# A decoder step on one core: the prompt's attention in units of two or four blocks of queries instead of single blocks

## The chip, the cores and the metric

The kernel is one program on one core of a Trainium2 chip. What counts is the time of the program on the device in microseconds (us), as the median of repeated runs. The engines are named as in the profile: PE is TensorE (matrix products and transposes; PEld is its loading of the stationary operand), DVE is VectorE, ACT is ScalarE, POOL is GpSimd, SP is SyncE (it issues the transfers).

## The reference

One layer of a decoder, for a prompt of 1024 tokens and 8 single sample tokens that share the weights, D_MODEL = 1024. The part that the change touches is the prompt's attention: 3 groups of 4 heads of 64 features, each with its own window and dilation.

```python
h = rms_norm(x, norm_mix_pre)
q, k, v, u, gates = jnp.split(h @ w_in, IN_SPLITS, axis=-1)
o, kv_bufs = attn_fn(q, k, v)
a = o.reshape(B, T, ATTN_OUT_W).astype(x.dtype) @ w_attn_out
c, conv_tail = conformer_conv(u, conv_hist, conv_w, conv_b, conv_ln_g, conv_ln_b, w_conv_out)
g = jax.nn.sigmoid(gates).reshape(B, T, 2, D_MODEL)
mix = (g[:, :, 0] * a + g[:, :, 1] * c) @ w_out
x = x + rms_norm(mix, norm_mix_post)
...
# band_dilated_attention, for each group (window, dilation): blocks of 128 queries,
# keys of the block itself and of the block before
s = jnp.einsum('bnqrhd,bnkrhd->bnrhqk', qb, kw) * SCALE + bias
s = jnp.where(valid[None, :, None, None], s, NEG)
lse = jax.nn.logsumexp(s, axis=-1)
pr = jnp.exp(s - lse[..., None])
o = jnp.einsum('bnrhqk,bnkrhd->bnqrhd', pr, vw)
```

After the mixing come a SwiGLU feed forward and an embedding gate; they take the second half of the time and are not touched.

## The kernel before

All big products keep f32 accuracy by splitting both operands into a high and a low part; `mm3` (lines 255 to 258) issues three products for each piece of 128 input features: L256 (high by high), L257 (low activations by high weights), L258 (high by low). `gemm_bank` fills one PSUM bank, 128 output features by one chunk of tokens, with 8 x 3 = 24 of these. The tokens come in three chunks `CH` of 384, 384 and 264 columns. So a "bank" below is 24 products of 384 or of 264 columns, and PE's work is a chain of banks.

Phase 1 (the first 500 us or so) makes the convolution's input (`u_pair`: 6 banks) and q, k, v for two heads at a time (`triple`: 9 banks; six triples, two for each of the three groups) in turns. A triple's attention runs beside the banks of the next steps. Its 8 blocks of 128 queries are each three steps (`attn_steps`):

- `qk`: the scores S of two heads, each into its own PSUM bank `S0`, `S1` (L592; the two heads lie on 64 partitions each), then on DVE bias and maximum (tile E from S) and on ACT the exponential (E from E),
- `pt`: the transposes of the probabilities, 128x128 each, into PSUM bank `PT` (L615), and ACT's copy to `PTs`,
- `pv`: the products with v into PSUM bank `O` (L630; each head uses 64 columns of the array), and ACT's copy to `oT`.

A block of group 0 or 1 that has a block before it has 256 keys (four transposes), the others 128 keys (two). The profile counts each f32 product of S and of O as two instructions, a transpose as one.

`attn_slot` is called after a bank, and on PE it puts three things next to each other: `pv` of the block two calls ago, `qk` of the new block, `pt` of the block one call ago. Such a stay of attention work between two products of a bank is called a visit below. There are 12 calls from one triple to the next; a triple needs 10. The last triple has only three banks left in `u_pair(7)`, so a loop after phase 1 issues the rest of its calls at once.

After phase 1 come 48 banks of the branch gates. Beside them, in a queue `bg` of generators that `pump` advances by a budget per bank, run the sample's attention, the rest of the convolution, `combine` (the three groups' results are read back from DRAM and weighted) and the convolution's layer norm. `misc()` hands out small PSUM banks from `mtags`, `bank()` the big ones from `gtags`.

PSUM has eight banks: three `g`, and `m`, `S0`, `S1`, `PT`, `O` with one buffer each. Scores, probabilities and small rows share a pool `sc` of four SBUF buffers. A scheduler places the instructions on each engine; the listings of order below show what it made.

Of the kernel before, what the change touches and what calls it, by code (L numbers as in the profile page):

```python
# [16 lines left out]
P = 128  # L17
# [9 lines left out]
# token chunks; the last holds 256 prompt tokens and the 8 sample tokens  # L27
# [9 lines left out]
# token chunks of the parts after the mix  # L37
# [17 lines left out]
def decoder_step(ctx: ExitStack, tc: tile.TileContext, ins, outs):  # L55
# [50 lines left out]
    class Engine:  # L106
        """An engine; its instructions stay in the order of emission while pinned[0] holds."""
# [59 lines left out]
    wq = []          # weight requests in the order of use: (dram view [128, n, 128], n)  # L167
# [75 lines left out]
    def finish(key):  # L243
        """The chains up to the one named."""
# [6 lines left out]
    def rng(c):  # L251
        """The token range of a chunk: its number among CH, or the range itself."""
# [7 lines left out]
    def gemm_bank(wi, xs, c, nk=KT, mid=None):  # L260
        """One bank: 128 output features by the tokens of chunk c."""
# [3 lines left out]
        for k in range(nk):  # L265
            if k == MID and mid is not None:
                mid()
# [7 lines left out]
    def gemm_bank_rows(wis, f, xs, c):  # L275
        """One bank, the weights held by rows: wis[k] has all output features of k."""
# [19 lines left out]
    def token_rstd(acc, c):  # L296
        """acc: SBUF [128, chunk] -> rstd columns of the tokens from the sums over the partitions."""
# [22 lines left out]
    class SumSq:  # L320
        """Sum of squares over feature tiles."""
# [25 lines left out]
    def split_scaled(src, g, hi, lo, c):  # L347
        """src * g per feature -> hi and lo."""
# [5 lines left out]
    def chunk_slots(name):  # L354
        """Four slots that hold a chunk of eight feature tiles, and the tiles' views."""
# [31 lines left out]
    # feed forward: the first tiles as they are, then pairs of gate and up  # L387
# [13 lines left out]
    # =====================================================================  # L401
    # start: loads, transposes, first norm, pp = p @ w_ple_proj
    # =====================================================================
# [44 lines left out]
    def setup():  # L448
# [25 lines left out]
        # relative position biases: table values by distance, as rows for skewed reads and as columns  # L474
# [41 lines left out]
        # biases of the sample's slots: the first 13 by distance, the tokens' own in every 16th row  # L516
# [55 lines left out]
    def o_view(o, g, blk):  # L572
        if g == 0:
            return o[:, blk * P:(blk + 1) * P]
        if g == 1:
            r, half = blk // 2, blk % 2
            return o[:, :S].rearrange("p (l r) -> p r l", r=4)[:, r, half * P:(half + 1) * P]
        j, r = blk // 4, blk % 4
        return o[:, :S].rearrange("p (l j i r) -> p j r i l", j=2, i=2, r=4)[:, j, r]

    def attn_steps(g, hp, qT, kT, vtok, oT, release):
        for blk in range(8):
            prev = (blk > 0) if g == 0 else (blk % 2 == 1) if g == 1 else False
            ko = 0 if prev else 128
            st = {}

            def qk(blk=blk, prev=prev, ko=ko, st=st):
                k0 = (blk - 1) * P if prev else blk * P
                nk = 256 - ko
                sp = [psa.tile([P, 512], F32, tag=f"S{h}", name=nm("S")) for h in range(2)]  # L590
                for h in range(2):
                    TE.matmul(sp[h][:, ko:256], qT[h * 64:(h + 1) * 64, blk * P:(blk + 1) * P],  # L592
                              kT[h * 64:(h + 1) * 64, k0:k0 + nk], start=True, stop=True)
                e = sc("E")
                for h in range(2):
                    head = hp * 2 + h
                    col = stat_col(g, blk, head)
                    if g < 2:
                        bv = biases[g][:, head * 256 + ko:(head + 1) * 256]
                    else:  # L600
                        bv = biases[g][:, head * P:(head + 1) * P]
                    ev = e[:, h * 256 + ko:(h + 1) * 256]
                    V.tensor_tensor_reduce(ev, sp[h][:, ko:256], bv, op0=ALU.add, op1=ALU.min,
                                           scale=-1.0, scalar=3e38, accum_out=NMs[g][:, col:col + 1])
                    A.activation(ev, ev, AF.Exp, scale=-1.0, bias=NMs[g][:, col:col + 1],
                                 accum_out=Ls[g][:, col:col + 1])
                st["e"] = e

            def pt(prev=prev, st=st):
                ps = psa.tile([P, 512], F32, tag="PT", name=nm("PT"))  # L610
                e = st["e"]
                for h in range(2):
                    for kb in range(0 if prev else 1, 2):
                        o = (h * 2 + kb) * P
                        TE.transpose(ps[:, o:o + P], e[:, o:o + P], ident)  # L615
                p = sc("PTs")
                if prev:
                    A.activation(p, ps, AF.Copy)
                else:
                    A.activation(p.rearrange("p (h b q) -> p h b q", h=2, b=2)[:, :, 1],  # L620
                                 ps.rearrange("p (h b q) -> p h b q", h=2, b=2)[:, :, 1], AF.Copy)
                st["p"] = p

            def pv(blk=blk, prev=prev, st=st):
                ps = psa.tile([P, 512], F32, tag="O", name=nm("O"))
                p = st["p"]
                kbs = range(0 if prev else 1, 2)
                for kb in kbs:
                    for h in range(2):
                        TE.matmul(ps[h * 64:(h + 1) * 64, :P], vtok[:, (blk - 1 + kb) * P + h * 64:(blk - 1 + kb) * P + (h + 1) * 64],  # L630
                                  p[:, (h * 2 + kb) * P:(h * 2 + kb + 1) * P],
                                  start=kb == kbs[0], stop=kb == kbs[-1])
                dst = o_view(oT, g, blk)
                src = ps[:, :P] if g < 2 else ps[:, :P].rearrange("p (i l) -> p i l", i=2)
                A.activation(dst, src, AF.Copy)
                if blk == 7:
                    SY.dma_start(d_o[g, hp], oT[:, :S])

            steps.append((qk, pt, pv))

    steps = deque()
    flight = deque()

    def attn_slot():
        new = steps.popleft() if steps else None
        if len(flight) > 1 and flight[1] is not None:
            flight[1][2]()
        if len(flight) > 1:
            flight.pop()
        if new is not None:  # L650
            new[0]()
        if flight and flight[0] is not None:
            flight[0][1]()
        flight.appendleft(new)

    def attn_busy():
        return bool(steps) or any(f is not None for f in flight)

# [1 line left out]
    def qkv_out(i):  # L660
        """The rows of the sample's tokens."""
# [12 lines left out]
    def kv_prompt_out(g, hp, dst, srcT):  # L674
        """The prompt's last rows, features by positions in the group's order."""
# [34 lines left out]
    def triple_done(i):  # L710
# [7 lines left out]
        attn_steps(g, hp, qT, kT, vtok, oT, None)  # L718
# [872 lines left out]
```

## Time and profile before

| | |
|---|---|
| time, median of 3 runs | 1733.48 us (1732.3 to 1733.5) |
| profiled execution, first to last instruction (span) | 1731.0 us |
| PE busy | 1712.0 us (99%) |
| DVE busy | 1220.9 us (71%) |
| ACT busy | 620.9 us (36%) |
| share of the chain that ended last | PE 96%, DVE 2%, issue 1% |

The profiled execution has no time of its own beside its span; the median of the timed runs lies 2.5 us above the span, which is what lies around the first and the last instruction. The chain that ended last is followed back from the end: 96% of it are PE's instructions, so time that PE gets free, or loses, is the kernel's time. A product's duration in the profile reaches from its start to its end in the pipeline, and neighbours overlap; what a product costs PE is the step from its start to the next start.

### The profile page before, as it was taken

What the parts mean: (1) busy time and instruction counts of PE and PEld (TensorE: products, weight loads), DVE (VectorE), ACT (ScalarE), POOL (GpSimd) and SP (SyncE); (2) the same over time, 40 slices, a digit from 0 to 9 for tenths busy, and PEclk for the clock granted to TensorE, in tenths of its full rate; (3) what the DMA queues carried; (4) which work ended last, traced back from release to release, by engine and by line L of the source; (5) the groups of instructions that cost most, each with busy time, mean ns of one, the idle gap of its engine ahead of it and who ended that gap; (6) DMA issues with size and microseconds to landing.
All of it is one profiled execution on the core that took longest, in us unless ns stands there. A gap on an engine that the chain in (4) does not pass through costs nothing.

```text
span 1731.0 us, 29699 instructions
## 1 busy us (share of the span) xinstructions
PE 1712.0 (99%) x12086; PEld 1661.9 (96%) x12086; DVE 1220.9 (71%) x2188; ACT 620.9 (36%) x1303; POOL 21.5 (1%) x29
## 2 busy tenths in 40 slices
PE   7999999999999999999999999999999999999999
PEld 7999998999989999999999999999999999999998
DVE  7899779858969696744577866666666545637863
ACT  6434434444352254323354432233332311213530
POOL 0000000000000000000000000000000000000000
PEclk9999999999999999999999999999999999999999
DMA  5231121121343322622252232233333532520411
GB/s 188 65 121 65 43 66 44 60 75 41 112 156 103 123 95 96 203 80 85 80 163 70 74 98 94 86 98 98 110 98 116 188 138 90 181 94 13 148 58 45
DMA packets 82254, 171.47 MB, mean 99 GB/s; under 512 B 11026, under 2 KB 52034, under 8 KB 81734
## 3 DMA queue, kind: packets, MB, share of 16 engines
q1 hardware_dynamic: 82118, 169.58, 29.8%
q8 instruction: 94, 1.54, 0.4%
q14 instruction: 42, 0.34, 0.1%
HBM read 133.04 MB, written 50.01 MB: 106 GB/s over the span
## 4 chain that ended last, share of the span: by engine, by line
PE 96%; DVE 2%; issue 1%; POOL 0%; DMA 0%; ACT 0%; POOLq 0%; SPq 0%; DVEq 0%
PE g L256 30%; PE g L258 30%; PE g L257 30%; PE S L592 1%; PE O L630 1%; PE PT L615 1%; DVE ogl L116 1%; PE m L317 0%; PE m L300 0%; PE m L690 0%; POOL r L116 0%; DVE acc L116 0%; DMA raw<-in_w_in_dram 0%; PE m L876 0%; DVE cs L116 0%
## 5 line engine op out<-in xcount | busy, mean ns | idle before, releaser
L256 PE MATMUL g<-hh,wh 128*128 128x384 f32 (+1 forms) x1200 | 393.3, 328 | 7.0 <-ACT wh L116 7.0
L257 PE MATMUL g<-hl,wh 128*128 128x384 f32 (+1 forms) x1200 | 386.6, 322 | 0.0
L258 PE MATMUL g<-hh,wl 128*128 128x384 f32 (+1 forms) x1200 | 386.3, 322 | 0.3 <-DVE wl L116 0.3
L116 DVE SCALAR_TENSOR_TENSOR y<-z,taps,y 128x1023 f32<-128x1023 f32 (+14 forms) x240 | 304.2, 1267 | 31.7 <-ACT y L116 26.1
L256 PEld LDWEIGHTS g<-hh,wh 128*128 128x128 f32 x1200 | 227.2, 189 | 10.7 <-ACT wh L116 7.0
L258 PEld LDWEIGHTS g<-hh,wl 128*128 128x128 f32 x1200 | 226.8, 189 | 1.5 <-DVE wl L116 0.8
L257 PEld LDWEIGHTS g<-hl,wh 128*128 128x128 f32 x1200 | 227.3, 189 | 0.9
L257 PE MATMUL g<-ul,wh 128*128 128x344 f32 x528 | 168.9, 320 | 0.0
L258 PE MATMUL g<-uh,wl 128*128 128x344 f32 x528 | 168.7, 320 | 0.0
L256 PE MATMUL g<-uh,wh 128*128 128x344 f32 x528 | 162.8, 320 | 0.6 <-DVE fa L116 0.6
L116 DVE TENSOR_TENSOR wl<-raw,wh 128x1024 fp32r<-128x1024 f32 x106 | 128.9, 1220 | 22.9 <-ACT wh L116 19.9
L116 DVE TENSOR_TENSOR pk<-pk,g 128x258 f32<-128x258 f32 x266 | 105.3, 420 | 52.4 <-PE g L258 36.9
L256 PE MATMUL g<-mh,wh 128*128 128x258 f32 x448 | 127.2, 285 | 0.0
L258 PE MATMUL g<-mh,wl 128*128 128x258 f32 x448 | 126.6, 283 | 0.0
L257 PE MATMUL g<-ml,wh 128*128 128x258 f32 x448 | 126.5, 283 | 0.0
L116 ACT ACTIVATE wh<-raw 128x1024 fp32r<-128x1024 f32 x106 | 110.7, 1052 | 6.5 <-DMA raw<-in_w_in_dram 4.2
L116 DVE TENSOR_TENSOR fa<-fa,g 128x344 f32<-128x344 f32 x96 | 47.1, 511 | 76.9 <-PE g L258 76.5
L258 PEld LDWEIGHTS g<-uh,wl 128*128 128x128 f32 x528 | 99.2, 188 | 0.0
L257 PEld LDWEIGHTS g<-ul,wh 128*128 128x128 f32 x528 | 99.2, 188 | 0.0
L256 PEld LDWEIGHTS g<-uh,wh 128*128 128x128 f32 x528 | 98.1, 188 | 0.9 <-DVE fa L116 0.9
L256 PE MATMUL g<-th,wbh 128*128 128x258 f32 x304 | 86.0, 283 | 0.0
L258 PE MATMUL g<-mh,wal 128*128 128x258 f32 x304 | 86.0, 283 | 0.0
(246 smaller groups left out, 3840.3 us busy)
## 6 DMA issues: line engine op xcount, KB each, us to landing
raw<-in_w_in_dram SPq DMA_DIRECT2D x50, 512.0 KB
raw<-in_w_ffn_in_dram SPq DMA_DIRECT2D x44, 512.0 KB
hr<-d_h SPq DMA_DIRECT2D x22, 516.0 KB
raw<-in_w_ffn_out_dram SPq DMA_DIRECT2D x22, 512.0 KB
d_h<-pk SPq DMA_DIRECT2D x38, 258.0 KB
out_kvs_dram<-in_cache_kv_w_dram SPq DMA_DIRECT2D x16, 510.0 KB
res<-in_xT_dram SPq DMA_DIRECT2D x8, 516.0 KB
d_x<-mo SPq DMA_DIRECT2D x32, 129.0 KB
```

Of the source, the lines that this page charges most:

```text
L116: ins = fn(*a, **k)
L256: TE.matmul(ps, hi_w, xh, start=first, stop=False)
L257: TE.matmul(ps, hi_w, xl, start=False, stop=False)
L258: TE.matmul(ps, lo_w, xh, start=False, stop=last)
L592: TE.matmul(sp[h][:, ko:256], qT[h * 64:(h + 1) * 64, blk * P:(blk + 1) * P], kT[h * 64:(h + 1) * 64, k0:k0 + nk], start=True, stop=True)
L615: TE.transpose(ps[:, o:o + P], e[:, o:o + P], ident)
L630: TE.matmul(ps[h * 64:(h + 1) * 64, :P], vtok[:, (blk - 1 + kb) * P + h * 64:(blk - 1 + kb) * P + (h + 1) * 64], p[:, (h * 2 + kb) * P:(h ...
```

## The change

A triple's attention goes in units: two blocks in groups 0 and 1 (four units for each triple), four blocks in group 2 (two units). A unit's scores fill the two banks `S0` and `S1` (up to 512 columns each), its probabilities are two halves with a tile E each, its results share the bank `O`. `attn_slot` now has two kinds of call. One issues `pv` of the unit in flight and `qk` of the next. The other issues the transposes of the first half, and leaves those of the second half to the next bank, whose `gemm_bank` issues them ahead of its sixth input piece (`MID` = 5, after 15 of the 24 products). The rest of the last triple is no longer issued at once after phase 1 but one call per bank in the gates' loop, and `combine`, `layer_norm` and the wider choice of PSUM banks follow when it is done.

```diff
     def gemm_bank(wi, xs, c, nk=KT, mid=None):
         t0, n = rng(c)
         ps = bank()
         sp = W(wi)
         for k in range(nk):
-            if k == MID and mid is not None:
-                mid()
+            if k == MID:
+                if mid is not None:
+                    mid()
+                if mids:
+                    mids.popleft()()
...
+    class Unit:
+        def __init__(self, g, hp, n, qT, kT, vtok, oT):
+            self.g, self.hp, self.n, self.ops = g, hp, n, (qT, kT, vtok, oT)
+            per = 2 if g < 2 else 4
+            self.blks = range(n * per, (n + 1) * per)
+            self.last = self.blks[-1] == 7
+            self.halves = (self.blks[:per // 2], self.blks[per // 2:])
+            self.e, self.p = [None, None], [None, None]
+        def prev(self, blk):
+            return (blk > 0) if self.g == 0 else (blk % 2 == 1) if self.g == 1 else False
+        def at(self, blk, h, kb):
+            half, i = divmod(blk - self.blks[0], len(self.halves[0]))
+            return half, ((h * 2 + kb) if self.g < 2 else (i * 2 + h)) * P
+        def qk(self):
+            g, hp = self.g, self.hp
+            qT, kT = self.ops[:2]
+            sp = [psa.tile([P, 512], F32, tag=f"S{h}", name=nm("S")) for h in range(2)]
+            cols, o = {}, 0
+            for blk in self.blks:
+                nk = 256 if self.prev(blk) else P
+                cols[blk] = o, nk
                 for h in range(2):
...
+                    TE.matmul(sp[h][:, o:o + nk], qT[h * 64:(h + 1) * 64, blk * P:(blk + 1) * P],
+                              kT[h * 64:(h + 1) * 64, (blk + 1) * P - nk:(blk + 1) * P], start=True, stop=True)
+                o += nk
+            for i, half in enumerate(self.halves):
+                self.e[i] = e = sc("E")
...
+        def pt(self, i):
+            ps = psa.tile([P, 512], F32, tag="PT", name=nm("PT"))
+            e, half = self.e[i], self.halves[i]
+            for blk in half:
                 for h in range(2):
...
+                    for kb in range(0 if self.prev(blk) else 1, 2):
+                        o = self.at(blk, h, kb)[1]
                         TE.transpose(ps[:, o:o + P], e[:, o:o + P], ident)
...
+            self.p[i] = p = sc("PTs")
+            if self.g == 2 or self.prev(half[0]):
+                A.activation(p, ps, AF.Copy)
+            else:
+                A.activation(p.rearrange("p (h b q) -> p h b q", h=2, b=2)[:, :, 1],
+                             ps.rearrange("p (h b q) -> p h b q", h=2, b=2)[:, :, 1], AF.Copy)
+        def pv(self):
+            g = self.g
+            vtok, oT = self.ops[2:]
+            ps = psa.tile([P, 512], F32, tag="O", name=nm("O"))
+            for i, blk in enumerate(self.blks):
+                kbs = range(0 if self.prev(blk) else 1, 2)
                 for kb in kbs:
                     for h in range(2):
...
+                        half, o = self.at(blk, h, kb)
+                        k0 = (blk - 1 + kb) * P + h * 64
+                        TE.matmul(ps[h * 64:(h + 1) * 64, i * P:(i + 1) * P], vtok[:, k0:k0 + 64],
+                                  self.p[half][:, o:o + P], start=kb == kbs[0], stop=kb == kbs[-1])
+            b0 = self.blks[0]
+            if g == 0:
+                dst, src = oT[:, b0 * P:(b0 + 2) * P], ps[:, :256]
+            elif g == 1:
+                dst, src = oT[:, :S].rearrange("p (l r) -> p r l", r=4)[:, b0 // 2], ps[:, :256]
+            else:
+                dst = oT[:, :S].rearrange("p (l j i r) -> p j r i l", j=2, i=2, r=4)[:, b0 // 4]
+                src = ps.rearrange("p (r i l) -> p r i l", r=4, i=2)
+            A.activation(dst, src, AF.Copy)
+            if self.last:
...
-    flight = deque()
+    flight = [None]
+    mids = deque()
     def attn_slot():
-        new = steps.popleft() if steps else None
-        if len(flight) > 1 and flight[1] is not None:
-            flight[1][2]()
-        if len(flight) > 1:
-            flight.pop()
-        if new is not None:
-            new[0]()
-        if flight and flight[0] is not None:
-            flight[0][1]()
-        flight.appendleft(new)
+        while mids:
+            mids.popleft()()
+        u = flight[0]
+        if u is not None and u.p[0] is None:
+            u.pt(0)
+            mids.append(lambda: u.pt(1))
+            return
+        if u is not None:
+            u.pv()
+        flight[0] = steps.popleft() if steps else None
+        if flight[0] is not None:
+            flight[0].qk()
     def attn_busy():
-        return bool(steps) or any(f is not None for f in flight)
+        return bool(steps) or flight[0] is not None
+    def attn_steps(g, hp, qT, kT, vtok, oT):
+        steps.extend(Unit(g, hp, n, qT, kT, vtok, oT) for n in range(4 if g < 2 else 2))
...
-        attn_steps(g, hp, qT, kT, vtok, oT, None)
+        attn_steps(g, hp, qT, kT, vtok, oT)
...
-    while attn_busy():
-        attn_slot()
...
-    mtags, gtags = deque(["m", "O"]), deque(["g", "S0", "g", "S1", "g", "PT"])
-    bg.append(combine())
-    bg.append(layer_norm())
+    def attn_done():
+        nonlocal mtags, gtags
+        mtags, gtags = deque(["m", "O"]), deque(["g", "S0", "g", "S1", "g", "PT"])
+        bg.append(combine())
+        bg.append(layer_norm())
+    rest = [attn_done]
...
                 A.activation(s[:, :n], ps[:, :n], AF.Sigmoid)
                 SY.dma_start(dst[i, :, t0:t0 + n], s[:, :n])
+                if attn_busy():
+                    attn_slot()
+                elif rest:
+                    rest.pop()()
                 pump(BUD)
```

The old closures `qk`, `pt`, `pv` that the diff removes stand in the listing above; in `qk` of a unit DVE's and ACT's instructions are the same as before, for each block and head of the first half and then of the second.

On PE, in the first triple (group 0), the work from one call of `attn_slot` over one bank to the next, before (g is the bank, hh and hl the activations' two parts, wh and wl the weights'):

```order
L615 MATMUL PT_1455<-ident,E_1385 128x128 x4
L256 MATMUL g_1466<-hh_113,wh_1264 128x384
...
L258 MATMUL g_1466<-hh_127,wl_1265 128x384
L630 MATMUL O_1492<-PTs_1460,vtok_1185 64x128 x4
L592 MATMUL S_1498<-kT_962,qT_787 128x256
L592 MATMUL S_1499<-kT_962,qT_787 128x256
L615 MATMUL PT_1507<-ident,E_1450 128x128 x4
L256 MATMUL g_1516<-hh_113,wh_1264 128x264
```

and now, at the same bank:

```order
L632 MATMUL PT_1449<-ident,E_1396 128x128 x4
L256 MATMUL g_1460<-hh_113,wh_1264 128x384
...
L632 MATMUL PT_1476<-ident,E_1401 128x128 x4
L256 MATMUL g_1460<-hh_123,wh_1264 128x384
...
L258 MATMUL g_1460<-hh_127,wl_1265 128x384
L650 MATMUL O_1493<-PTs_1454,vtok_1185 64x128 x4
L650 MATMUL O_1493<-PTs_1481,vtok_1185 64x128 x4
L604 MATMUL S_1503<-kT_962,qT_787 128x256
L604 MATMUL S_1504<-kT_962,qT_787 128x256
```

Every bank's end had one visit of three kinds; now a visit has either transposes alone, or O and S of a whole unit, and the second transposes stand alone inside the bank, nine products ahead of the O that needs them. (S of the unit's second block follows as two more rows like the last two.)

On ACT, at the same place, before (PTs is the copy of the transposes, wh the splitting of the next weights, qT a bank's result, oT the copy of O):

```order
L116 ACTIVATE PTs_1460<-PT_1455 128x512
L116 ACTIVATE wh_1570<-raw_1262 128x1024
L116 ACTIVATE E_1450,l_108<-E_1450,nm_105 128x256
L116 ACTIVATE qT_1406<-g_1466 128x384
L116 ACTIVATE oT_1200<-O_1492 128x128
L116 ACTIVATE PTs_1512<-PT_1507 128x512
L116 ACTIVATE E_1502,l_108<-E_1502,nm_105 128x256 x2
```

and now:

```order
L116 ACTIVATE PTs_1454<-PT_1449 128x512
L116 ACTIVATE wh_1560<-raw_1262 128x1024
L116 ACTIVATE PTs_1481<-PT_1476 128x512
L116 ACTIVATE qT_1415<-g_1460 128x384
L116 ACTIVATE oT_1200<-O_1493 128x256
L116 ACTIVATE E_1509,l_108<-E_1509,nm_105 128x256 x2
L116 ACTIVATE E_1514,l_108<-E_1514,nm_105 128x256 x2
```

The copy of the second half stands right behind the copy of the first, or behind one splitting of weights, and ahead of the next bank's result; oT's copy takes a whole unit.

## Rows read from the trace of the kernel before

**Rows 1.** The page: the span.

```profile
span 1731.0 us, 29699 instructions
```

**Rows 2.** Busy time in phase 1: length, then each engine, clock, DMA share, GB/s.

```profile
100.00:500.00 400.00, 399.94 (x2699) 364.56 (x2699) 335.56 (x469) 177.03 (x459) 0.00 (x0) 1.00 0.21 69
```

**Rows 3.** PE's timeline around a visit of O, S and transposes (start, length).

```profile
139.67 0.29 PE L257 MATMUL g<-hl,wh 128*128 128x264 f32 x1
139.80 0.28 PE L258 MATMUL g<-hh,wl 128*128 128x264 f32 x1
140.01 0.66 PE L630 MATMUL O<-PTs,vtok 128*64 128x128 f32 x8
140.60 0.70 PE L592 MATMUL S<-kT,qT 64*128 64x256 f32 x4
141.23 0.66 PE L615 MATMUL PT<-ident,E 128*128 128x128 f32 x4
...
141.90 0.34 PE L257 MATMUL g<-hl,wh 128*128 128x384 f32 x1
```

**Rows 4.** The group of O's products: count, busy us, mean ns of one.

```profile
L630 PE MATMUL O<-PTs,vtok 128*64 128x128 f32 x280 | 25.9, 290 | 0.1
```

**Rows 5.** PE's timeline around transposes alone, twice, inside a bank.

```profile
176.16 0.34 PE L258 MATMUL g<-hh,wl 128*128 128x384 f32 x1
176.34 0.60 PE L690 MATMUL m<-ident,vT 128*128 128x128 f32 x4
...
176.95 0.34 PE L257 MATMUL g<-hl,wh 128*128 128x384 f32 x1
...
177.31 0.34 PE L256 MATMUL g<-hh,wh 128*128 128x384 f32 x1
177.62 0.66 PE L690 MATMUL m<-ident,vT 128*128 128x128 f32 x4
```

**Rows 6.** PE's timeline around a visit of S alone.

```profile
186.49 0.34 PE L258 MATMUL g<-hh,wl 128*128 128x384 f32 x1
186.76 0.49 PE L592 MATMUL S<-kT,qT 64*128 64x128 f32 x4
...
187.46 0.33 PE L257 MATMUL g<-hl,wh 128*128 128x384 f32 x1
```

**Rows 7.** PE's timeline around a visit of S and transposes.

```profile
191.31 0.34 PE L258 MATMUL g<-hh,wl 128*128 128x384 f32 x1
191.58 0.70 PE L592 MATMUL S<-kT,qT 64*128 64x256 f32 x4
192.21 0.44 PE L615 MATMUL PT<-ident,E 128*128 128x128 f32 x2
...
192.61 0.29 PE L257 MATMUL g<-hl,wh 128*128 128x264 f32 x1
```

**Rows 8.** PE's timeline around a visit of O alone.

```profile
234.00 0.33 PE L258 MATMUL g<-hh,wl 128*128 128x384 f32 x1
234.27 0.66 PE L630 MATMUL O<-PTs,vtok 128*64 128x128 f32 x8
...
235.14 0.34 PE L257 MATMUL g<-hl,wh 128*128 128x384 f32 x1
```

**Rows 9.** ACT's timeline beside rows 5: the copy of the transposes, then weights.

```profile
176.97 0.60 ACT L116 ACTIVATE vtok<-m 128x512 f32<-128x512 f32 x1 [2.02 <-PE m L690]
177.47 1.05 ACT L116 ACTIVATE wh<-raw 128x1024 fp32r<-128x1024 f32 x1
```

**Rows 10.** PE's timeline: the scores whose exponentials came latest.

```profile
119.48 0.70 PE L592 MATMUL S<-kT,qT 64*128 64x256 f32 x4
```

**Rows 11.** ACT's timeline: the last exponential's end of rows 10, then of rows 7.

```profile
123.69 0.19 ACT L116 ACTIVATION_READ_ACCUMULATOR E<-E,nm 128x1 f32 x1
194.09 0.19 ACT L116 ACTIVATION_READ_ACCUMULATOR E<-E,nm 128x1 f32 x1
```

**Rows 12.** DVE's longest wait between 500 and 690 us: total, times, longest.

```profile
DVE m L116 <- PE m L769: 9.1, 1, 9.1
```

More of the change, by code (lines that the diff above doesn't have):

```diff
@@ L570, in stat_col @@
         return (blk // 4) * 16 + head * 4 + blk % 4
[L572 to L590, printed above, removed]
-                for h in range(2):
-                    TE.matmul(sp[h][:, ko:256], qT[h * 64:(h + 1) * 64, blk * P:(blk + 1) * P],
-                              kT[h * 64:(h + 1) * 64, k0:k0 + nk], start=True, stop=True)
-                e = sc("E")
-                for h in range(2):
[L596 to L614, printed above, removed]
-                        TE.transpose(ps[:, o:o + P], e[:, o:o + P], ident)
[L616 to L627, printed above, removed]
@@ new lines, in decoder_step @@
+    class Unit:
[19 more added lines that the diff above has]
+                cols[blk] = o, nk
+                for h in range(2):
+                    TE.matmul(sp[h][:, o:o + nk], qT[h * 64:(h + 1) * 64, blk * P:(blk + 1) * P],
[4 more added lines that the diff above has]
+                for blk in half:
+                    o, nk = cols[blk]
+                    for h in range(2):
+                        head = hp * 2 + h
+                        col = stat_col(g, blk, head)
+                        if g < 2:
+                            bv = biases[g][:, (head + 1) * 256 - nk:(head + 1) * 256]
+                        else:
+                            bv = biases[g][:, head * P:(head + 1) * P]
+                        c1 = self.at(blk, h, 1)[1] + P
+                        ev = e[:, c1 - nk:c1]
+                        V.tensor_tensor_reduce(ev, sp[h][:, o:o + nk], bv, op0=ALU.add, op1=ALU.min,
+                                               scale=-1.0, scalar=3e38, accum_out=NMs[g][:, col:col + 1])
+                        A.activation(ev, ev, AF.Exp, scale=-1.0, bias=NMs[g][:, col:col + 1],
+                                     accum_out=Ls[g][:, col:col + 1])
+        def pt(self, i):
+            ps = psa.tile([P, 512], F32, tag="PT", name=nm("PT"))
+            e, half = self.e[i], self.halves[i]
+            for blk in half:
+                for h in range(2):
+                    for kb in range(0 if self.prev(blk) else 1, 2):
+                        o = self.at(blk, h, kb)[1]
+                        TE.transpose(ps[:, o:o + P], e[:, o:o + P], ident)
+            self.p[i] = p = sc("PTs")
[10 more added lines that the diff above has]
+                kbs = range(0 if self.prev(blk) else 1, 2)
@@ L628, in pv @@
                 for kb in kbs:
                     for h in range(2):
[L630 to L635, printed above, removed]
@@ L636, in pv @@
-                if blk == 7:
-                    SY.dma_start(d_o[g, hp], oT[:, :S])
-            steps.append((qk, pt, pv))
+                        half, o = self.at(blk, h, kb)
[7 more added lines that the diff above has]
+                dst, src = oT[:, :S].rearrange("p (l r) -> p r l", r=4)[:, b0 // 2], ps[:, :256]
+            else:
+                dst = oT[:, :S].rearrange("p (l j i r) -> p j r i l", j=2, i=2, r=4)[:, b0 // 4]
+                src = ps.rearrange("p (r i l) -> p r i l", r=4, i=2)
@@ L641, in decoder_step @@
+            A.activation(dst, src, AF.Copy)
+            if self.last:
+                SY.dma_start(d_o[g, self.hp], oT[:, :S])
     steps = deque()
-    flight = deque()
+    flight = [None]
+    mids = deque()
     def attn_slot():
-        new = steps.popleft() if steps else None
-        if len(flight) > 1 and flight[1] is not None:
-            flight[1][2]()
-        if len(flight) > 1:
-            flight.pop()
-        if new is not None:
-            new[0]()
-        if flight and flight[0] is not None:
-            flight[0][1]()
-        flight.appendleft(new)
+        while mids:
[10 more added lines that the diff above has]
+            flight[0].qk()
```

## The prediction

> **What bounds the kernel now.** I read the page first, for the span [rows 1], then busy time by stretches. Between 100 and 500 us, where the attention lies, PE is busy 399.94 of 400 us at a granted clock of 1.00 (2.4 GHz), DVE 335.56 (84%), ACT 177.03 (44%) [rows 2]. With the chain of the front's table (96% PE) this means that PE sets the end, and that the change is worth what it saves on PE, less new waits. The number of PE's products is the same in both programs (by the listings of order: 96 of S, 140 of O, 140 transposes). What can differ is what a visit costs beyond its products, so next I read PE's timeline around each kind of visit.
>
> **How a visit is costed.** From the start of the last product before it to the start of the second product after it; without a visit that would be two steps of a bank. A step is 0.18 us with 384 columns (two steps from 176.95 to 177.31) [rows 5] and 0.13 with 264 [rows 3]. What is left is the attention's own products and an overhead. The products: a transpose takes 0.11, since four last 0.66 and two 0.44 [rows 3, 7]. An instruction of O takes 0.053: eight last 0.66, one lasts 0.29, so (0.66 - 0.29) / 7 [rows 3, 4]. For S I estimate the same per column: 0.053 with 128 columns, 0.106 with 256.
>
> - O, S and four transposes: 141.90 - 139.80 = 2.10; less 0.13 and 0.18 that is 1.79; products 8 x 0.053 + 4 x 0.106 + 4 x 0.11 = 1.28; overhead 0.51 [rows 3].
> - S alone: 0.97 - 0.36 - 0.21 = 0.40 [rows 6]. S and two transposes: 1.30 - 0.18 - 0.13 - 0.42 - 0.22 = 0.35 [rows 7]. O alone: 1.14 - 0.36 - 0.42 = 0.36 [rows 8].
> - Transposes alone inside a bank, those of v: 176.95 - 176.16 = 0.79, less 0.36 and 0.44: nothing [rows 5]. Their second group began at 177.62 where a step after 177.31 would be 177.49, so 0.13 late; it waited for its PSUM bank, whose copy ended at 177.57 [rows 5, 9].
>
> So O and S cost PE something on the way in and out, and transposes next to a bank's products don't. What the rows show as a later start (O begins 0.21 after the product ahead of it, not 0.13 [rows 3]) the Trainium skill states as a rule: in "TensorEngine Tiling (Array Packing)", section "Tiling Modes", changing the way in which the array is divided drains the engine, changing the tile alone doesn't. By that rule a transpose, which uses the undivided array as a bank does, is free beside a bank, and a visit of O and S has the same three changes as one of O, S and transposes; at 0.51 for it the sum below would be 15.7 in place of 15.0.
>
> **The change, part by part.** *Fewer visits with O and S.* By the order on PE, before has 6 visits of S, 6 of S and transposes, 33 of O, S and transposes, 7 of O and transposes, 6 of O, and 4 mixed ones in the burst after the last triple. After has 6 of S, 14 of O and S, 6 of O, and 40 of transposes alone. Before: 6 x 0.40 + 6 x 0.35 + 33 x 0.51 + 7 x 0.35 (taken like S and transposes) + 6 x 0.36 + 1.42 (the mixed ones: 0, 0.40, twice 0.51) = 27.4 us. After: 6 x 0.40 + 14 x 0.56 + 6 x 0.36 + 40 x 0 = 12.4 us. The visit of O and S doesn't exist before: not under 0.51 (no fewer kinds to enter than with transposes behind) and not over 0.40 + 0.36 = 0.76 (each by itself); I take 0.51 - 0.35 + 0.40 = 0.56, the three kinds with S's other exit. **Saved: 15.0 us.** Bounds: 0.7 more at 0.51, 2.8 less at 0.76; transposes alone up to 0.13 late each would be 5.2 less. I take none, since the first group in rows 5 had none.
>
> *The second half's short way.* New is that O needs a copy of transposes issued only nine products earlier. Behind O in PE's queue stand the next unit's S and then every bank, so all of PE would wait. The round trip is in the trace: transposes end at 176.34 + 0.60 = 176.94, ACT copies from 176.97 for 0.60, the next user of the bank starts at 177.62 [rows 5, 9]: 0.68 after the end. O is due after nine steps less the 0.16 by which the last transpose (0.27 long, a step of 0.11) overlaps them: 1.46 us with 384 columns, 1.0 with 264. Free, if ACT is. The order on ACT puts the copy right behind the first half's copy, or behind one splitting of weights of 1.05 us [rows 9] that itself stands right behind the first copy, fifteen products earlier, so I take 0. One splitting just in front would make it 1.73: late by 0.27 or 0.73, mean 0.5, 10 us in 20 units. That is a rival below.
>
> *Eight or sixteen scores at once.* DVE and ACT do the same instructions as before. The first transposes follow one bank after S. The slowest scores began at 119.48 and had their last exponential at 123.69 + 0.19, after 4.4 us [rows 10, 11], with pieces of the convolution in between; those of rows 7 took 2.7 [rows 7, 11]. With S's own 0.85 and 24 steps, the transposes come 4.1 us after S begins behind a bank of 264 columns (4 units) and 5.2 behind 384. So 0 to 4 x 0.3 us; I take 0. ACT saves 28 copies of O and 8 of transposes; it is 44% busy, so that is worth nothing here.
>
> *The last triple and what follows it.* Its rest moves from a burst to the first two gate banks; the store of its result to DRAM stands a gate's store later on SP's queue and is read only by `combine`, so it costs nothing. `combine` and the layer norm enter their queue three banks later, behind the sample's attention and the convolution that still stand there; their order on PE is the same. In that stage DVE waited 9.1 us for PE [rows 12], so it can follow a PE that comes 15 us earlier for most of the way. Everything after 500 us then moves forward by the same time.
>
> **Sum.** Span 1731.0 - 15.0 = 1716.0. The median of the runs lies 2.5 us above the profiled span; 1733.5 - 15.0 = **1718.5 us**.
>
> **Rivals.**
>
> - *Transposes alone pay an entry like the others.* If each of the 40 cost the 0.36 of O alone, 14.4 of the 15.0 would go: 1732.9, no change. For it: they are 40 new visits. Against it: the first group of rows 5.
> - *The copy of the second half comes late (slower).* O waits in 20 units. It decides at 15.0 / 20 = 0.75 us per unit. With two pieces like the splitting of weights ahead of each copy (0.68 + 2.1 = 2.8 after the transposes) O is late by 1.3 or 1.8, mean 1.6, 32 us: 1750. For it: ACT's pieces are long and its queue goes in order. Against it: the order on ACT, where at most one such piece stands there. In "TensorEngine Tiling (Array Packing)", section "Performance Considerations", the Trainium skill warns of this: when the array gets faster, copying out of PSUM may become the bottleneck. No row here shows it yet, since a copy had a whole bank's time.
> - *DVE doesn't follow.* 335.6 us of work then fall on 385 us, 87%. If it kept its old times up to the sample's attention, PE would wait there for 15.0 - 9.1 = 5.9 us: 1724.4.
>
> **How the numbers follow.** The forecast, 1716 to 1721.5: 0.70. The bounds of its terms together, up to 1727: 0.10. DVE doesn't follow, about 1724: 0.05. Transposes pay: 0.08. The copy comes late: 0.07. The range of 1715.5 to 1727 leaves the last two out, and takes in the bounds: 15.0 - 5.2 - 2.8 = 7.0 us saved is 1726.5, and 15.7 less a run's spread of some 1 us is about 1716. A measurement here can tell some 0.2%, 3.5 us, from no change: faster 0.85, the same 0.08, slower 0.07.
>
> **What would show it.** PE busy still near 99% with a span of about 1716; in the timeline visits of O and S with an overhead near 0.56 and transposes between two steps of a bank without one; no idle time of PE ahead of O and of the transposes by the waits; the transposes of the sample's attention some 15 us earlier than before. Wrong it would be if PE's waits name ACT's PTs or E, if transposes inside a bank cost 0.1 or more beyond 0.11 each, or if time is lost after 500 us.

## The result, and the profile after

The changed kernel takes 1721.26 us (median of 5 runs, 1718.97 to 1722.75) against 1733.5 us before (1732.3 to 1737.81, 5 runs): 0.9923 of it, with a 95% interval of 0.9911 to 0.9935. The forecast was 1718.5 us. The profiled span fell by 14.1 us, from 1731.0 [rows 1] to 1716.9, where 15.0 had been forecast; the profiled run is the lowest of the five, which is why the medians differ by less, 12.2 us. The page after, span and engines' busy time:

```profile
span 1716.9 us, 29651 instructions
PE 1697.4 (99%) x12086; PEld 1662.6 (97%) x12086; DVE 1220.1 (71%) x2188; ACT 617.1 (36%) x1265; POOL 21.4 (1%) x29
```

PE is as full as before with the same number of instructions, and busy 14.6 us less. In phase 1, busy time by stretch (columns as in [rows 2]) shows no idle time to speak of, and no wait of PE at the attention's lines stands in the list of waits between 100 and 500 us:

```profile
100.00:485.00 385.00, 384.86 (x2695) 365.16 (x2694) 331.23 (x464) 173.38 (x421) 0.00 (x0) 1.00 0.21 70
```

So the saving must lie in PE's steps. PE's timeline around one unit's second transposes and its visit of O and S (start, length), which answers to [rows 3, 5]:

```profile
141.87 0.34 PE L258 MATMUL g<-hh,wl 128*128 128x384 f32 x1
142.04 0.60 PE L632 MATMUL PT<-ident,E 128*128 128x128 f32 x4
...
142.65 0.34 PE L257 MATMUL g<-hl,wh 128*128 128x384 f32 x1
...
143.87 0.34 PE L258 MATMUL g<-hh,wl 128*128 128x384 f32 x1
144.14 1.09 PE L650 MATMUL O<-PTs,vtok 128*64 128x128 f32 x16
145.16 1.14 PE L604 MATMUL S<-kT,qT 64*128 64x256 f32 x8
...
146.50 0.34 PE L257 MATMUL g<-hl,wh 128*128 128x384 f32 x1
```

The transposes: 142.65 - 141.87 = 0.78, less two steps (0.36) and four transposes (0.44): nothing, as in [rows 5]. O and S: 146.50 - 143.87 = 2.63, less 0.36, 16 x 0.053 and 8 x 0.106: 0.57. Costed in this way, all visits from the first S to the sample's attention, those of v's transposes [rows 5] with them, add up to 28.5 us before and 14.1 after. After, these are 6 of S at 0.42, 14 of O and S at 0.58, 6 of O at 0.36, 0.5 for the 40 visits of transposes (-0.02 to 0.01 each but for four, which cost 1.0 together) and 0.9 for v's transposes, which before cost the same. Without v's transposes, which the forecast's sum leaves out, it is 27.6 before and 13.3 after.

A second reading needs no costing: PE's time from the first S to the first transpose of the sample's attention (L769 before, L800 now), from the lines' first and last starts. Before, 504.5 - 114.7 = 389.8 us:

```profile
L592 PE MATMUL S<-kT,qT x192: 272/373/481, 114.7 to 486.1; 64*128 64x128 f32 x104, 64*128 64x256 f32 x88
L769 PE MATMUL m<-ident,smx x1: 271/271/271, 504.5 to 504.5; 128*4 128x128 f32 x1
```

After, 489.3 - 113.7 = 375.6 us:

```profile
L604 PE MATMUL S<-kT,qT x192: 272/373/481, 113.7 to 467.0; 64*128 64x128 f32 x104, 64*128 64x256 f32 x88
L800 PE MATMUL m<-ident,smx x1: 272/272/272, 489.3 to 489.3; 128*4 128x128 f32 x1
```

That is 14.2 us less. Both readings serve for every experiment below; overheads are the sums of the first reading, v's transposes with them, the stage is that of the second reading, ratios are to the kernel before on the same chip.

| kernel | overheads, us | stage, us | median, us | ratio, 95% interval |
|---|---|---|---|---|
| before | 28.5 | 389.8 | 1733.5 | |
| after | 14.1 | 375.6 | 1721.26 | 0.9923, 0.9911 to 0.9935 |
| after again (e6) | 14.1 | 375.6 | 1719.96 | 0.9922, 0.9910 to 0.9934 |
| transposes alone, single blocks (e1) | 30.0 | 391.7 | 1734.82 | 1.0004, 0.9994 to 1.0014 |
| second transposes 3 products ahead of O (e2) | 17.5 | 378.7 | 1723.91 | 0.9930, 0.9914 to 0.9946 |
| last triple in a burst (e3) | 15.2 | 376.4 | 1720.09 | 0.9908, 0.9893 to 0.9924 |
| second transposes right ahead of O (e7) | 25.2 | 386.7 | 1730.93 | 0.9980, 0.9971 to 0.9990 |
| three more steps (e5) | 11.7 | 373.2 | 1716.91 | 0.9903, 0.9889 to 0.9918 |
| 72 products that nobody reads, after 500 us (e4) | 14.1 | 375.6 | 1747.73 | 1.0068, 1.0052 to 1.0083 |

### The profile page after: what moved, and what is told of

Same layout as the page of the kernel before. It is cut to its first block, busy times and chain, and to the rows that moved or that the text cites. A ratio compares the mean times of both kernels' runs of the same rounds, so it can differ in the third digit from the quotient of the medians.

```text
span 1716.9 us, 29651 instructions
## 1 busy us (share of the span) xinstructions
PE 1697.4 (99%) x12086; PEld 1662.6 (97%) x12086; DVE 1220.1 (71%) x2188; ACT 617.1 (36%) x1265; POOL 21.4 (1%) x29
## 4 chain that ended last, share of the span: by engine, by line
PE 92%; DVE 5%; issue 1%; ACT 1%; DMA 1%; POOL 0%; POOLq 0%; SPq 0%; ACTq 0%; DVEq 0%
PE g L256 29%; PE g L258 29%; PE g L257 29%; DVE y L116 3%; PE O L650 1%; PE S L604 1%; PE PT L632 1%; DVE ogl L116 1%; DVE wl L116 1%; PE m L320 0%; PE m L303 0%; POOL r L116 0%; DMA res<-d_x 0%; PE m L907 0%; PE m L721 0%
## 5 line engine op out<-in xcount | busy, mean ns | idle before, releaser
L257 PE MATMUL g<-tl,wbh 128*128 128x258 f32 x304 | 86.0, 283 | 0.0
```

The costliest lines, as they stand in the source:

```text
L257: TE.matmul(ps, hi_w, xl, start=False, stop=False)
```

## The experiments

**e1: the transposes alone, without units.** To the kernel before:

```diff
+            if k == MID:
+                if mid is not None:
+                    mid()
+                if mids:
+                    mids.popleft()()
...
         if flight and flight[0] is not None:
-            flight[0][1]()
+            mids.append(flight[0][1])
```

> The kernel before with one part of the change alone: single blocks as before, but the transposes of a block leave the visit of O and S and stand by themselves inside the next bank, ahead of its sixth piece. Theory (what costs PE is a visit with O and S, as often as there are such visits; transposes beside a bank's products are free): nothing is gained. By the order on PE there are 12 visits of S, 30 of O and S, 11 of O and a handful of mixed ones; at 0.41, 0.58 and 0.36 us (the overheads in the trace of the changed kernel) and 4 us for the mixed ones that makes some 30 us against 27.4 before: 2.5 us slower, about 1736. Rival (the gain came from parting the transposes from O and S, or from the place inside the bank): most of the 14 us appear already here, 1726 or less. Second rival (each visit costs alike, transposes too): 42 more visits at 0.36 make 15 us more, 1749.

Measured: no gain; the stage is 1.9 us longer, the overheads 1.5 us more, and the ratio's interval takes in 1. PE's timeline of one block:

```profile
145.29 0.34 PE L258 MATMUL g<-hh,wl 128*128 128x384 f32 x1
145.56 0.66 PE L633 MATMUL O<-PTs,vtok 128*64 128x128 f32 x8
146.15 0.70 PE L595 MATMUL S<-kT,qT 64*128 64x256 f32 x4
...
147.06 0.34 PE L257 MATMUL g<-hl,wh 128*128 128x384 f32 x1
```

147.06 - 145.29 = 1.77, less 0.36, 0.42 and 0.42: 0.57. The visit costs no less than with four transposes behind S (0.51, [rows 3]), and the 42 visits of transposes alone cost -0.4 us in all. So parting the transposes gains nothing by itself, and they don't pay an entry either: both rivals fall. As e3 leaves the spread of the last triple at most 1 us, what carries the gain is that a visit serves two or four blocks.

**e4: the price by itself.** To the changed kernel, 72 products that nobody reads, inside the banks of the convolution's output product, in turn one on 64 partitions as S (L264), one on 64 columns as O (L266), one undivided (L268), a transpose (L270), and two of 64 columns side by side (L272, L273):

```diff
+            if dose and k in (2, 4, 6):
+                one(dose[0], dose[1])
+                dose[1] += 1
...
+        if i % 5 == 0:
+            TE.matmul(pd[:, :P], ident[:64, :], ident[:64, :], start=True, stop=True)
+        elif i % 5 == 1:
+            TE.matmul(pd[:64, :P], ident[:, :64], ident, start=True, stop=True)
+        elif i % 5 == 2:
+            TE.matmul(pd[:, :P], ident, ident, start=True, stop=True)
+        elif i % 5 == 3:
+            TE.transpose(pd[:, :P], ident, ident)
+        else:
+            TE.matmul(pd[:64, :P], ident[:, :64], ident, start=True, stop=True)
+            TE.matmul(pd[64:, :P], ident[:, 64:], ident, start=True, stop=True)
```

> The changed kernel with 72 products added that nobody reads: in the 24 banks of the convolution's output product, ahead of the third, fifth and seventh piece of each, in turn one f32 product with 64 partitions (as S), one with 64 columns (as O), one undivided with 128 by 128, one transpose, and a pair with 64 columns side by side; each of 128 columns, some 14 of each kind. Theory (leaving and entering the undivided array costs PE, about 0.2 us each way): overheads beyond the products' own time of 0.40 (as S), 0.36 (as O), 0 (undivided), 0 (transpose) and 0.36 us (the pair); with own times of 0.11 to 0.21 us about 30 us in all, 1751. Rival (it is the f32 product after the rounded-f32 products of the bank that costs, not the division): the undivided product has 0.4 too, 1757. Second rival (a visit costs nothing by itself, what was seen around O and S were waits for other engines): overheads of 0 for all kinds, 1734.

PE's timeline of the first three kinds and of the last:

```profile
700.14 0.33 PE L258 MATMUL g<-sh,wl 128*128 128x384 f32 x1
700.40 0.48 PE L264 MATMUL m<-ident 64*128 64x128 f32 x2
700.81 0.44 PE L256 MATMUL g<-sh,wh 128*128 128x384 f32 x1
701.09 0.34 PE L257 MATMUL g<-sl,wh 128*128 128x384 f32 x1
...
701.80 0.33 PE L258 MATMUL g<-sh,wl 128*128 128x384 f32 x1
702.07 0.43 PE L266 MATMUL m<-ident 128*64 128x128 f32 x2
...
702.72 0.34 PE L257 MATMUL g<-sl,wh 128*128 128x384 f32 x1
...
703.41 0.34 PE L258 MATMUL g<-sh,wl 128*128 128x384 f32 x1
703.59 0.39 PE L268 MATMUL m<-ident 128*128 128x128 f32 x2
...
703.99 0.34 PE L257 MATMUL g<-sl,wh 128*128 128x384 f32 x1
...
706.91 0.34 PE L258 MATMUL g<-sh,wl 128*128 128x384 f32 x1
707.18 0.32 PE L272 MATMUL m<-ident 128*64 128x128 f32 x1
707.18 0.32 PE L273 MATMUL m<-ident 128*64 128x128 f32 x1
...
707.82 0.34 PE L257 MATMUL g<-sl,wh 128*128 128x384 f32 x1
```

From the product before to the second after, less two steps: the one like S 0.95 - 0.36 = 0.59, the one like O 0.92 - 0.36 = 0.56, undivided 0.58 - 0.36 = 0.22, the pair side by side 0.91 - 0.36 = 0.55. By means over all of a kind these are 0.60, 0.55, 0.21 and 0.55, and the transpose comes to 0.10. An undivided f32 product therefore starts one step after the bank's product and costs what its two instructions last; one with 64 partitions starts 0.26 after it, is followed 0.41 later, and costs 0.37 more than the undivided one. The pair costs the price of one. Less an own time of 0.21, the overheads are within 0.03 of the theory's (0.40, 0.36, 0, 0, 0.36), and the whole, 15 x (0.60 + 0.55) + 14 x (0.21 + 0.10 + 0.55) = 29.3 us, is near the spans' 1746.7 - 1716.9 = 29.8 (by medians of one chip, 1747.73 to e3's 1720.09, 27.6). Both rivals fall: it is neither the f32 product behind the bank's rounded ones (their operands have the type fp32r of [rows 9]), nor a wait for another engine, but the divided array.

**e2: the short way made shorter.**

```diff
-                if mids:
-                    mids.popleft()()
+            if k == 7 and mids:
+                mids.popleft()()
```

> The changed kernel with the transposes of the second half ahead of the eighth input piece of the bank instead of the sixth: O is due three products after them instead of nine. Theory (the copy's round trip is 0.68 us after the transposes' end; with nine products O is due 1.0 or 1.46 us after it and nothing waits): O is now due 0.38 us (384 columns) or 0.23 us (264) after the transposes' end, so it waits 0.30 or 0.45 us in each of 20 units, 7.5 us; with O, S, O, S in place of O, S in a few visits 1 to 2 us more: about 1730. Rival (ScalarE takes the copy late in any case, behind its queue): with one splitting of weights in front it is 1.3 to 1.5 us in each unit, 28 us, 1749. Second rival (the scheduler's order hides it, with S ahead of O): no change, 1721.

Measured: 3.1 us in the stage, 3.3 in the overheads, under half of what the theory expected. PE's timeline of a visit behind 384 columns and of one behind 264:

```profile
145.09 0.60 PE L632 MATMUL PT<-ident,E 128*128 128x128 f32 x4
...
145.87 0.34 PE L258 MATMUL g<-hh,wl 128*128 128x384 f32 x1
146.14 1.09 PE L650 MATMUL O<-PTs,vtok 128*64 128x128 f32 x16
```
```profile
123.73 0.44 PE L650 MATMUL O<-PTs,vtok 128*64 128x128 f32 x4
124.10 0.70 PE L604 MATMUL S<-kT,qT 64*128 64x256 f32 x2
124.73 0.66 PE L650 MATMUL O<-PTs,vtok 128*64 128x128 f32 x8
125.31 1.13 PE L604 MATMUL S<-kT,qT 64*128 64x256 f32 x6
```

In the first, the copy would be ready 0.68 after the transposes' end, at 146.37, and O begins at 146.14 without a gap in its 16 instructions: its first eight need only the first half's copy, and last 0.43. The theory had let all of O wait. In the second the first half is four instructions long, and the scheduler put S between; such visits (4) cost 1.13 to 1.34 instead of 0.58. Two things are in that. There are five changes between the array's divisions in place of three, and S loses its pairs: the instructions of the two heads, on 64 partitions each, otherwise start in twos within 0.01 us of each other and share a step of 0.21 with 256 columns, while here the two at 124.10 start one after the other and last 0.70, as long as four do in [rows 3]. By the starts in the trace this is 1.4 us in the four visits. So the place of the second half is worth 3 us, and 2.6 of them are these four visits: changes between O and S and parted pairs of S, not a plain wait.

**e7: no products between.** The call in `gemm_bank` is left out, so that the next call of `attn_slot` issues the second half itself:

```diff
-                if mids:
-                    mids.popleft()()
```

> The changed kernel with the transposes of the second half right ahead of O, with no products of a bank between them. The scheduler's order then puts S between the two halves of O in 14 of the 20 units (transposes, O, S, O, S in 12) and products of a bank between them in the other 6. Theory (each change between the three ways of dividing the array costs 0.19 us, 0.58 / 3, and O's first half covers 0.43 us of the copy's round trip): 5 changes in 12 visits, 4 in 2, 2 in 12 visits of O, so 11.6 + 1.5 + 4.3 us and 3.5 us for S alone and group 2's waits, 21 us in place of 14; with 0 to 0.2 us of waiting in each unit 7 to 10 us slower than the changed kernel. Rival (a visit costs once, whatever changes within it): 6 more visits of O at 0.36, 2 us slower. Second rival (PE waits the copy's whole round trip of 0.68 us in each unit, and changes cost too): 20 us slower.

Measured: 11.1 us more in the stage than the changed kernel (1730.93 to 1719.96 by medians on one chip: 11.0), a little above the theory's 7 to 10, far from either rival. One of the 12 visits, and ACT's copy of its second half, which stood behind a splitting of weights and ended at 148.04, 1.53 after the transposes:

```profile
147.45 0.59 ACT L116 ACTIVATE PTs<-PT 128x512 f32<-128x512 f32 x1
```
```profile
145.74 0.34 PE L258 MATMUL g<-hh,wl 128*128 128x384 f32 x1
145.91 0.60 PE L630 MATMUL PT<-ident,E 128*128 128x128 f32 x4
146.44 0.66 PE L648 MATMUL O<-PTs,vtok 128*64 128x128 f32 x8
147.03 1.13 PE L602 MATMUL S<-kT,qT 64*128 64x256 f32 x6
148.09 0.66 PE L648 MATMUL O<-PTs,vtok 128*64 128x128 f32 x8
148.68 0.70 PE L602 MATMUL S<-kT,qT 64*128 64x256 f32 x2
...
149.58 0.34 PE L257 MATMUL g<-hl,wh 128*128 128x384 f32 x1
```

149.58 - 145.74 = 3.84, less 0.36, 0.44, 0.85 and 0.85: 1.34. Over the 12 the overhead goes from 0.93, which is five changes at 0.19, to 1.62, 1.23 on average. Of the 3.5 us above 0.94 most is again S without its pairs: by the starts in the trace, four instructions of S stand alone in eight of these visits, which costs 0.42 in six and 0.21 in two, 2.9 us in all; here the two of S at 148.68 last the 0.70 of two pairs. No expectation had that; without it the 11.1 would be 8.2, within the theory's 7 to 10. The list of waits names ACT's PTs for 1.4 us, 1.2 of them in the two visits of four changes. So not visits as such are paid for, but changes of the array within them, and pairs that are parted.

**e3: the last triple in a burst.**

```diff
-    rest = [attn_done]
+    while attn_busy():
+        attn_slot()
+    attn_done()
+    rest = []
```

> The changed kernel with the rest of the last triple issued at once after phase 1, as before the change, so that the small PSUM banks, the combination and the layer norm follow three banks earlier. Theory: only the last unit's second transposes and its O are without banks between them; two copies' round trips of 0.68 us, less what the order puts between, so 0.5 to 1.4 us slower, about 1722; the part of the change that spreads the last triple carries at most a tenth of the gain. Rival (the spreading of the last triple carries much of the gain, because the burst stops PE until the exponentials are done, 4.4 us): 1725 or more.

Measured: 0.8 us in the stage, 1.0 in the overheads, as the theory has it; the time itself (0.9908, its interval overlapping the changed kernel's) doesn't tell the two apart. PE waited 0.3 us for E, not 4.4.

**e5: three more steps; e6: the changed kernel again.** In e5 the transposes of group 2 go one bank later, a triple's last O waits for the next S, and v's second transposes use the bank O (cut to these places):

```diff
+        if u is not None and u.g == 2 and u.wait:
+            u.wait = False
+            return
...
+        if u is not None and not steps and u.hp + 2 * u.g < 5:
+            return
...
-            ps = misc()
+            ps = psa.tile([P, 512], F32, tag="O", name=nm("m")) if b0 else misc()
```

> The changed kernel with three more steps on the same theory. The last O of a triple waits for the first S of the next triple, so that 5 visits of S (0.41 us) and 5 of O (0.36) become 5 of O and S (0.58): 0.95 us less. In group 2 the transposes come one bank later, so that they don't wait for the exponentials of sixteen scores (in the trace of the changed kernel 0.32 and 0.50 us late, and 0.15 us behind them): 0.95 us less. The second transposes of v go to the bank O and don't wait for the copy of the first (0.2 us late in each of 5 triples): 1.0 us less. Theory (only what PE loses between products counts): 2.9 us less of overhead in phase 1, so a time 2 to 3 us under that of the changed kernel, if VectorE, which had 1.8 us in hand at the sample's attention, follows. Rival (VectorE doesn't follow any more): the same time as the changed kernel, with a new wait of PE at the sample's attention. Second rival (the O that waits holds buffers of probabilities, and small rows wait for these): slower by 1 us or more.

> The changed kernel as it is, beside the others on the same chip. Every theory: 0.992 of the kernel before. Read from its trace: the sum of the overheads in phase 1 (14.1 us in the first trace) should come out within 0.3 us again; where the granted clock falls to half after 500 us may differ, and with it the span by 1 to 2 us, if that fall isn't the program's.

Measured: the second trace of the changed kernel gives the same stage and the same overheads to 0.1 us, and by the medians on this chip it is 14.2 us faster than the kernel before (1734.14 to 1719.96). e5 takes 2.4 us off the stage; its median is 3.05 us lower on the same chip, though the ratios' intervals still touch. Of the 2.9 us expected of the overheads 2.4 came: the merged visits cost 0.57 to 0.61 and the late transposes are gone but for 0.2 us, but VectorE has nothing left in hand, and the first transposes of the sample's attention, for which PE waited for DVE's maxima smx, start 0.49 after the product ahead of them, where the changed kernel had one step of 0.18:

```profile
486.97 0.34 PE L258 MATMUL g<-hh,wl 128*128 128x384 f32 x1
487.46 0.27 PE L807 MATMUL m<-ident,smx 128*4 128x128 f32 x1
```

So the first rival of e5 begins there, with 0.3 us. (The transposes that follow are 0.24 late in e5 and in the changed kernel alike.)

## Why the prediction was right, step by step

*The bound and the costing.* Right: PE sets the end, and a visit's overhead times its count explains the time. Without v's transposes the trace before sums to 27.6 (forecast 27.4), the one after to 13.3 (forecast 12.4), so 14.3 us were saved where 15.0 were forecast. That the sum before fits so well is in part luck: the four mixed visits of the burst cost 2.2 where 1.4 was taken, and the seven of O and transposes 0.30 each where 0.35 was taken. O and S cost 0.58 where 0.56 was taken, within its bounds of 0.51 to 0.76; e1 shows the same price with single blocks, e4 the same for products put elsewhere. The rule of the Trainium skill in "TensorEngine Tiling (Array Packing)", section "Tiling Modes", that a change of the division drains the engine, agrees with e4 (0.4 us in and out with 64 partitions, nothing undivided) and e7 (0.93 for five changes where neither waits nor single products of S add to them); the prediction's reading of it for the new visit, 0.51 as for the old one with three changes too, is 0.07 too low.

*Transposes alone are free.* Right: 41 of the 42 visits in e1, 36 of the 40 after. "Eight or sixteen scores at once" was taken as 0 with a bound of 1.2 us; this is the term that was too small. The step took the slowest block of before, 4.4 us from S to its last exponential, for a whole unit's first half. In group 2 that half needed 5.9, from 390.37 to 396.31, and its transposes came 5.4 after S: they waited for E, 0.32 and 0.50 us, and the ones behind them were late by 0.15 together: 1.0 us. PE's rows of S and of the first transposes, and two of ACT's rows beside it (start, length, idle time before and its releaser):

```profile
390.37 1.16 PE L604 MATMUL S<-kT,qT 64*128 64x128 f32 x16
...
395.76 0.94 PE L632 MATMUL PT<-ident,E 128*128 128x128 f32 x4
```
```profile
393.37 1.28 ACT L116 ACT_TABLE_LOAD   x1 [6.70 <-DVE nm L116]
...
396.12 0.19 ACT L116 ACTIVATION_READ_ACCUMULATOR E<-E,nm 128x1 f32 x1
```

ACT waited for DVE's maxima (DVE was at a piece of the convolution until 393.08) and loaded a table for 1.28 us; four transposes take 0.60 elsewhere and 0.94 here. e5 moved them by one bank, and the wait was gone but for 0.2 us.

*The second half's short way.* Right that it costs nothing: ACT's copy ended 0.68 to 0.70 after the transposes in all 20 units. In the unit of the first timeline the transposes ended at 142.64, and the copy at 143.34:

```profile
142.74 0.60 ACT L116 ACTIVATE PTs<-PT 128x512 f32<-128x512 f32 x1 [2.11 <-PE PT L632]
```

The step's working was off on the safe side: O is due later than the 1.0 and 1.46 us that were written, by the 0.43 of its first half (e2). The slower rival was therefore farther off than its price said. Its mechanism exists: in e7 four of the copies stood behind other work of ACT and ended 1.5 to 1.8 us after the transposes. The warning of the Trainium skill in "TensorEngine Tiling (Array Packing)", section "Performance Considerations", that copying out of PSUM may become the bottleneck once TensorE is faster, is shown by no run here: the late copies of e7 lasted their usual 0.6 us and were late by their place in ACT's queue, and in the changed kernel none was late.

*The last triple.* Taken as costing nothing, with 1.42 us for the old burst; e3 finds 0.8 to 1.0 us for a burst of units.

*DVE follows, and what comes after 500 us.* Right, with less in hand than "for most of the way" says: the wait of [rows 12] shrank to

```profile
DVE m L116 <- PE m L800: 1.8, 1, 1.8
```

The transposes of the sample's attention come at 489.3, 15.2 us earlier, 1.0 of which the profiled run had before any attention (first S at 113.7, before 114.7). Behind them 1.2 us were lost again, which the granted clock accounts for. Stretches after, then the one of the fall in e6, the same program, then those before:

```profile
580.00:590.00 10.00, 9.56 (x37) 7.68 (x38) 8.84 (x11) 1.06 (x1) 0.00 (x0) 0.72 0.59 204
590.00:600.00 10.00, 10.00 (x59) 9.08 (x57) 6.67 (x7) 1.93 (x3) 0.00 (x0) 0.94 0.25 86
```
```profile
510.00:520.00 10.00, 8.74 (x52) 8.46 (x51) 10.00 (x11) 2.16 (x3) 0.00 (x0) 0.83 0.35 111
```
```profile
520.00:530.00 10.00, 9.01 (x51) 8.72 (x50) 10.00 (x12) 1.44 (x2) 0.00 (x0) 0.93 0.25 86
530.00:540.00 10.00, 10.00 (x61) 10.00 (x60) 9.59 (x9) 4.28 (x6) 0.00 (x0) 0.90 0.56 174
```

After, 10 x (0.28 + 0.06) = 3.4 us of full clock are missing, in e6 1.7 (its clock is 1.00 from 580 to 600 us), and before 1.7 as well. So e6, with the same loss as before, should lose nothing behind the transposes, and it doesn't: they come 14.5 us earlier than before, and its span of 1716.5 is 14.5 us shorter. So 14.2 us is the change's, and what the profiled spans add or take is a start and a fall of the clock that the same program has now here, now there. *The rivals* that transposes pay and that DVE doesn't follow fell with e1 and with the stage's 14.2 us.

## What to carry to other kernels

Count on PE not the products but the changes between ways of dividing the array: here each costs 0.19 us, a transpose or an undivided f32 product beside a bank costs its own time alone, and merging visits is worth the changes that it takes away, as long as the work beside them keeps its distance and products on two halves of the array stay next to each other (e7). Making O and S undivided with zeros would by an estimate, which no run here tests, not pay: two heads side by side cost one price (e4), so O's 280 instructions [rows 4] alone, at 0.053 each 14.8 us of steps, would double, for less than 12.8 us of overheads of O and S in all. Read a stage of the trace whose ends the engine sets, since it repeats to 0.1 us where the span moves by 1 to 4 (after, 1716.9 to 1720.7).

## What the runs showed of the hardware that was not expected

An f32 product among rounded-f32 ones costs nothing but its own 0.21 us (e4). Two products on the two column halves run at the price of one, 0.55 us with their entry (e4), and two on the two row halves, as S of two heads, share a step of 0.21 us (an instruction of 256 columns) that one alone takes too (e2, e7). Between 500 and 630 us the granted clock fell to half, its level of 1.2 GHz, for some microseconds in every profiled run: after, it is 0.50 from 585 to 590 us, and in e5 products of 384 columns then last 0.52 us in place of 0.34. It fell behind the small products of the sample's attention (before, e2, e4, e6), ahead of which PE had stood idle for about 1 us, or behind those of the combination (after, e1, e3, e7), in e5 behind both. As PE stood idle for 0.7 to 1.0 us ahead of the sample's attention in after, e1, e3 and e7 too, without a fall, what decides between the two places stays open. By the clock of stretches of 10 us that is a loss of 1.7 us (before, e4, e6) to 6.9 us (e5: 0.83, 0.64 and 0.84 in three of them), and it differed between two runs of one program; e5's profiled span of 1717.2 us holds 5.2 us more of it than e6's 1716.5.
